# Routed experts: the steps between two arms move into the arms, and the arms are entered without hints

## The chip, the cores and the metric

The program runs on one core of one Trainium2 chip. The metric is the device time of one execution in microseconds (us), the median of several. The core has five engines, each with its own instruction stream: TensorE (PE in the rows; PEld is its loading of weights), VectorE (DVE), ScalarE (ACT), GpSimd (POOL) and SyncE (SP, here the engine that issues most DMAs). An engine takes its instructions in order and waits on semaphores for the others.

## What is computed

A trunk of two layers over 256 latent and 256 context tokens of width 1024: a recurrent mixer and a dense feed-forward network in the first layer, a pooling mixer and routed experts in the second. The change touches only the routed experts (latent tokens alone, each token goes to 2 of 8):

```python
def moe_swiglu(h, router_w, router_b, w1, w3, w2):
    logits = (h @ router_w) + router_b
    top_logit, top_idx = lax.top_k(logits, TOP_K)
    top_p = jax.nn.softmax(top_logit, axis=-1)
    gates = jnp.einsum('btk,btke->bte', top_p, jax.nn.one_hot(top_idx, N_EXPERTS))
    y = jnp.zeros_like(h)
    for e in range(N_EXPERTS):
        y = y + gates[..., e:e + 1] * swiglu(h, w1[e], w3[e], w2[e])
    return y
...
x = layer_norm(DN_ALPHA * x + gt2 * moe_swiglu(x * (1.0 + sc2) + sh2), ln_g, ln_b)
```

All data is float32. Each expert has 17.3 MB of weights (w1, w3: 1024 x 1408, w2: 1408 x 1024).

## The kernel before

The experts are worked one after the other. How many tokens an expert got is known only on the chip, so each expert is a switch with five arms: two blocks of up to 128 tokens, both full; a full and a small block (up to 64); one full block (`Full`); one small one (`Small`); one of up to 32 tokens (`Tiny`). The count, compared with 32, 64, 128 and 192, picks the arm. TensorE, VectorE, ScalarE and SyncE each load the number of the arm into a register and branch by themselves; each arm is its own stretch of code on each engine, and all arms of an expert are followed by one common block. With this input the experts 0, 4, 5 and 7 take the `Tiny` arm, 1, 2 and 6 the `Full` one, 3 the arm with a full and a small block.

Ahead of an arm stand three steps, which this text calls so:

- *gather*: 16 products of the normalised rows `z` with a one-hot matrix `oh` pick the expert's tokens, turned, into PSUM; eight affine steps (`affine3`, four on VectorE, four on ScalarE) bring them to `xg`.
- *turn*: two transposes and a copy make `ohT`, which the adding back needs.
- *adding back* (`scatter`): four products of `ohT` with the arm's result `yf`, and four additions with the gate on VectorE into `acc`.

The one-hot matrix of the next expert is made on GpSimd. In the kernel before these steps lie in the common block between two arms, in the order gather for e, turn for e, adding back of e - 1, then the branch into e's arm. `fetch` puts a hint behind the first instruction of the gather on each of three engines: it loads the register there and names the switch that will be taken (`tc.switch_hint`). SyncE has none. Every arm begins, in both kernels, with a hint for its own end.

An arm multiplies in 13 stages in the order `u0 u1 u2 d0 u3 d1 u4 d2 u5 d3 t5 d4 d5` (u: up, d: down, t: turning the last hidden piece). A full block multiplies in split form: data and weights are cut into a high and a low part of type fp32r, and three products (`mm3`, L237) take the place of one in float32. The weights are split while they are used: for each piece of 512 columns ScalarE makes the high part (L1284, `wh`) and VectorE the low one (L1285, `wl`), with four buffers each. The data are split in `begin` (`high`, `low`, into `xs3`). In the arm with one full block the first half of `u0` isn't split but multiplied in float32 (L1835), which the None in `split` does; `Tiny` (L1756, L1774) and `Small` (L1791, L1805) multiply in float32 throughout.

Weights come in pieces of 1 MB through 19 slots in a ring; SyncE issues the load of piece g + 19 when piece g has been used (`pload`). The scheduler of the language orders the instructions of one block of code on each engine, and doesn't move any across a branch.

Of the kernel before, what the change touches and what calls it, by code (L numbers as in the profile page):

```python
# [12 lines left out]
ALU = mybir.AluOpType  # L13
# [187 lines left out]
def kernel(ctx: ExitStack, tc: tile.TileContext, I: dict, out: bass.AP, dbg=None):  # L201
# [1076 lines left out]
    def split_weight(raw):  # L1278
# [9 lines left out]
        def at(a, o, n):  # L1288

            i = a * raw.shape[2] + o  # L1290
            return [v[:, i % PART:i % PART + n] for v in parts[i // PART]]
# [366 lines left out]
    def gather(oh, xg, n=P):  # L1658

        work = {}  # L1660
        for d4 in range(2):
            pt = gen()
            for j in range(4):
                dt = 4 * d4 + j
                for t in range(2):
                    i = nc.tensor.matmul(pt[:, P * j:P * j + n], lhsT=z[:, t, P * dt:P * dt + P], rhs=oh[:, t, 0:n], start=(t == 0), stop=(t == 1))  # L1666
                    work.setdefault(i.ins.engine, []).append(i.ins)
            for j in range(4):
                i = affine3(4 * d4 + j, xg[:, 4 * d4 + j], pt[:, P * j:P * j + n])
                work.setdefault(i.ins.engine, []).append(i.ins)  # L1670
        return work
# [22 lines left out]
    def fetch(e, work):  # L1694

        for g, w in work.items():
            n = len(nc.cur_bb.bb.instructions)
            tc.switch_hint({g: vals[e]}, len(BOUNDS) + 1, f"arm{e}")
            for i in list(nc.cur_bb.bb.instructions)[n:]:
                tc.add_manual_dep(i, w[0].name, S.same, reason="order")  # L1700
            for j in w[1:]:
                tc.add_manual_dep(j, i.name, S.same, reason="order")

    onehot(0, 0, nc.vector, oh)
    fetch(0, gather(oh, xgs[0]))
    turn_oh(oh, ohT[0])
    ex, p1_, sm = rt("ex", [P, 2, 1]), rt("p1_", [P, 2, 1]), rt("sm", [P, 2, 1])
# [105 lines left out]
    class Full(Block):  # L1813


        def high(self, sl):
            nc.scalar.activation(xs3[0][:, sl], self.xg[:, sl], AF.Copy)

        def low(self, sl):
            nc.vector.tensor_tensor(xs3[1][:, sl], self.xg[:, sl], xs3[0][:, sl], op=ALU.subtract)  # L1820

        def begin(self, two):
            for h in range(2):
                sl = slice(4 * h, 4 * h + 4)
                self.high(sl)
                if two or h:
                    self.low(sl)

        def up(self, c, sp):
            self.ps = gen()  # L1830
            ps = self.ps[:, 0:512 if c < 5 else 256]
            for k in range(DT):
                v = None if self.b else sp[c](k)
                if v is None:
                    nc.tensor.matmul(ps, lhsT=self.xg[:, k], rhs=self.w["u", c](k), start=(k == 0), stop=(k == DT - 1))  # L1835
                    if k == 3 and not self.b:
                        self.low(slice(0, 4))
# [255 lines left out]
```

## Time and profile before

| | us |
|---|---|
| median of 3 runs | 1413.09 |
| lowest, highest | 1411.98, 1415.58 |
| profiled execution | 1417.35 |
| its span, first to last instruction | 1415.5 |
| PE busy in the span | 1150.7 (81%) |
| DVE busy | 915.2 (65%) |
| ACT busy | 622.5 (44%) |
| POOL busy | 343.0 (24%) |

The profiled execution is a single one; its time stands 4.26 us above the median. A row of the trace gives the start in us from the beginning of the span, the duration, the engine, the line, what is written and read, and in brackets how long the engine had been idle before and what ended that. "issue" there means that the engine waited for nothing that the profile shows. Durations of single instructions overlap a little, so that x4 with 2.49 means one about every 0.62 us. The routed experts fill the span from about 944 to 1404 us.

### The profile page before, as it was taken

Reading aid. Unit: us, or ns where it says so; the run is one execution under the profiler, and the core shown is the slowest. Engines: PE = TensorE matmul, PEld = TensorE weight load, DVE = VectorE, ACT = ScalarE, POOL = GpSimd, SP = SyncE. Lnnn points to the kernel's source line nnn. Section 1 sums busy time; section 2 is a strip of 40 time slices with the busy share of each in tenths; the row PEclk is TensorE's granted clock in tenths of the full one; section 3 lists DMA queues with packets and bytes.
Section 4 is the critical chain, followed back from the end, with each engine's and each line's share of the span. In section 5 each row is a group of like instructions: output and inputs, shape, how many; then the busy total and the mean of one; then the engine's idle time right before and its main releaser. Section 6 shows DMA issues by size and latency. Waiting matters only on the chain.

```text
span 1415.5 us, 26008 instructions
## 1 busy us (share of the span) xinstructions
PE 1150.7 (81%) x9885; PEld 879.2 (62%) x9885; DVE 915.2 (65%) x1821; ACT 622.5 (44%) x1330; POOL 343.0 (24%) x467
## 2 busy tenths in 40 slices
PE   1589659977888788689689998957989899968886
PEld 0267448955566566554489898855768655646663
DVE  7897417857867776654977777662869545622764
ACT  3443218466655675221244444321758345311750
POOL 6341130037705667011622222050000000000000
PEclk8699879988967799589889999979999799998998
DMA  8225645566657446362935455739959354499950
GB/s 355 92 88 193 200 139 175 160 172 188 182 105 200 102 132 176 68 208 76 391 120 180 173 183 194 291 142 389 383 217 361 132 179 151 170 415 416 398 219 32
DMA packets 131594, 288.37 MB, mean 204 GB/s; under 512 B 63536, under 2 KB 90288, under 8 KB 108208
## 3 DMA queue, kind: packets, MB, share of 16 engines
q1 hardware_dynamic: 128064, 278.50, 56.4%
q10 hardware_dynamic: 3312, 7.31, 1.4%
q8 instruction: 95, 1.56, 0.5%
q14 instruction: 123, 1.01, 0.2%
HBM read 273.17 MB, written 12.60 MB: 202 GB/s over the span
## 4 chain that ended last, share of the span: by engine, by line
PE 38%; DVE 4%; DMA 4%; issue 3%; ACT 1%; POOL 0%; DVEq 0%; ACTq 0%; SPq 0%; POOLq 0%
PE pb L237 24%; PE pb L1756 3%; DMA arena<-in_moe_w13b_dram 3%; PE pb L1666 2%; PE pb L1791 2%; PE pb L1729 2%; PE pb L1835 1%; PE pb L1774 1%; DMA slot<-in_moe_w_dram 1%; PE pb L1805 1%; DVE wl L1285 1%; DVE usl L1433 1%; ACT wh L1284 0%; DVE x L1731 0%; DVE lnst L1360 0%
## 5 line engine op out<-in xcount | busy, mean ns | idle before, releaser
L1285 DVE TENSOR_TENSOR wl<-arena,wh 128x512 fp32r<-128x512 f32 x262 | 211.2, 832 | 77.7 <-ACT wh L1284 76.5
L1284 ACT ACTIVATE wh<-arena 128x512 fp32r<-128x512 f32 x262 | 160.3, 628 | 120.8 <-PE pb L237 106.7
L237 PE MATMUL pb<-usl,wh 128*128 128x256 f32 x352 | 101.0, 288 | 12.6 <-DVE usl L1433 12.6
L237 PE MATMUL pb<-ush,wh 128*128 128x256 f32 x352 | 100.0, 286 | 1.7 <-DVE fsg L1451 1.7
L237 PE MATMUL pb<-ush,wl 128*128 128x256 f32 x352 | 100.0, 285 | 0.0
L1656 POOL TENSOR_SCALAR oh<-consts,consts 128x128 f32<-128x128 f32 x14 | 8.3, 605 | 355.2 <-PE pb L1666 345.3
L1285 DVE TENSOR_TENSOR wl<-slot,wh 128x512 fp32r<-128x512 f32 x122 | 79.7, 687 | 22.3 <-ACT wh L1284 21.9
L1284 ACT ACTIVATE wh<-slot 128x512 fp32r<-128x512 f32 x122 | 75.0, 629 | 29.8 <-PE pb L237 26.6
L1097 DVE SCALAR_TENSOR_TENSOR sv<-sv,wc,pb 64x64 f32<-64x64 f32 x192 | 45.8, 278 | 57.9 <-issue 23.7
L1072 ACT ACTIVATE sv<-pb 64x128 f32<-64x128 f32 x128 | 34.6, 271 | 101.7 <-PE pb L1066 96.5
L237 PEld LDWEIGHTS pb<-usl,wh 128*128 128x128 f32 x352 | 68.2, 194 | 16.2 <-DVE usl L1433 14.0
L1315 POOL TENSOR_TENSOR arena<-arena,rows 128x2048 f32<-128x2048 f32 x11 | 52.0, 4729 | 103.8 <-DMA arena<-in_ffn_w_dram 103.8
L944 POOL TENSOR_TENSOR arena<-arena 128x56 f32<-128x56 f32 (+22 forms) x155 | 70.7, 456 | 12.2
L237 PEld LDWEIGHTS pb<-ush,wh 128*128 128x128 f32 x352 | 67.7, 193 | 4.0 <-DVE fsg L1451 1.9
L237 PE MATMUL pb<-wl,xsh 128*128 128x512 f32 (+1 forms) x180 | 69.7, 387 | 0.0
L237 PE MATMUL pb<-wh,xsh 128*128 128x512 f32 (+1 forms) x180 | 69.2, 387 | 0.0
L237 PEld LDWEIGHTS pb<-ush,wl 128*128 128x128 f32 x352 | 68.2, 194 | 1.2
L237 PE MATMUL pb<-wh,xsl 128*128 128x512 f32 (+1 forms) x180 | 67.0, 372 | 0.0
L1764 DVE TENSOR_TENSOR mh<-mh,pb 64x128 f32<-64x128 f32 (+1 forms) x24 | 7.0, 291 | 81.3 <-PE pb L1774 38.1
L853 PE MATMUL pb<-arena 128*128 128x192 f32 x256 | 52.3, 356 | 6.3 <-DVE arena L788 3.1
L853 PEld LDWEIGHTS pb<-arena 128*128 128x128 f32 x256 | 44.8, 204 | 11.3 <-DVE arena L788 3.8
L942 POOL TENSOR_TENSOR arena<-arena 128x126 f32<-128x126 f32 (+22 forms) x93 | 43.2, 464 | 27.8 <-DMA arena<-s 21.2
(446 smaller groups left out, 3089.0 us busy)
## 6 DMA issues: line engine op xcount, KB each, us to landing
slot<-in_moe_w_dram SPq DMA_DIRECT2D x62, 1024.0 KB, 11.2
arena<-in_moe_w_dram SPq DMA_DIRECT2D x58, 1024.0 KB, 6.7
arena<-in_ffn_w_dram SPq DMA_DIRECT2D x33, 1024.0 KB, 4.8
arena<-in_ada_w_dram SPq DMA_DIRECT2D x28, 512.0 KB, 4.3
ada<-in_ada_w_dram SPq DMA_DIRECT2D x28, 512.0 KB, 4.8
hvr<-in_w_rkv_dram SPq DMA_DIRECT2D x12, 1024.0 KB, 10.6
wr<-in_ada_w_dram SPq DMA_DIRECT2D x10, 1024.0 KB, 8.7
sv<-v_d SPq DMA_DIRECT2D x128, 64.0 KB, 2.8
```

Of the source, the lines that this page charges most:

```text
L237: i = nc.tensor.matmul(ps, lhsT=a[x], rhs=b[y], start=start and n == 0, stop=stop and n == 2)
L853: nc.tensor.matmul(pb(g)[:, 192 * j:192 * j + 192], lhsT=kap_b[kap.i][:, c + j].rearrange("p h t -> p (h t)"), rhs=kbi_b[kbi.i][:, c + j])
L942: eng.tensor_tensor(mv, T[:, cs, j:j + 1].to_broadcast([P, nci, nii]), X[:, ii, j].unsqueeze(1).to_broadcast([P, nci, nii]), op=ALU.mult)
L944: eng.tensor_tensor(T[:, cs, ii], T[:, cs, ii], mv, op=ALU.subtract)
L1072: nc.scalar.activation(sv_(si, d, 1)[zd(d)], bank[zd(d), 0:128], AF.Copy, scale=-1.0)
L1097: nc.vector.scalar_tensor_tensor(t[:, x], sv_(si, d, 0)[zd(d), x], wc_b[wc.i][zd(d), h, si:si + 1], bank[zd(d), 128 + 64 * h:192 + 64 * h] ...
L1284: nc.scalar.activation(hi, r[:, o:o + PART], AF.Copy)
L1285: nc.vector.tensor_tensor(lo, r[:, o:o + PART], hi, op=ALU.subtract)
L1315: S.behind(nc.gpsimd.tensor_tensor(w, w, gt.unsqueeze(1).to_broadcast(w.shape), op=ALU.mult))
L1666: i = nc.tensor.matmul(pt[:, P * j:P * j + n], lhsT=z[:, t, P * dt:P * dt + P], rhs=oh[:, t, 0:n], start=(t == 0), stop=(t == 1))
L1729: nc.tensor.matmul(ps, lhsT=ohT[:, t], rhs=yf[:, 512 * j:512 * j + 512], start=True, stop=True)
L1756: nc.tensor.matmul(ps[32 * g:32 * g + 32, 0:P], lhsT=xg[:, k, 0:32], rhs=m[g], start=(k == 0), stop=(k == DT - 1))
```

## The change

The common block between arms keeps only the register load and the branch, and the one-hot on GpSimd. Gather and turn for expert e + 1, and the splitting of its data (`halves`, now in every arm), stand in expert e's arm behind stage t5; adding back of e - 1 stands at the start of e's arm if that begins with a full block, else behind u1. All of `u0` is split, so the float32 product in single full arms goes. The three hints go.

```diff
     def gather(oh, xg, n=P):
 
-        work = {}
         for d4 in range(2):
...
             for j in range(4):
-                i = affine3(4 * d4 + j, xg[:, 4 * d4 + j], pt[:, P * j:P * j + n])
-                work.setdefault(i.ins.engine, []).append(i.ins)
-        return work
+                affine3(4 * d4 + j, xg[:, 4 * d4 + j], pt[:, P * j:P * j + n])
+
+    def halves():
+
+        for h in range(2):
+            sl = slice(4 * h, 4 * h + 4)
+            nc.scalar.activation(xs3[0][:, sl], xgs[0][:, sl], AF.Copy)
+            nc.vector.tensor_tensor(xs3[1][:, sl], xgs[0][:, sl], xs3[0][:, sl], op=ALU.subtract)
...
     onehot(0, 0, nc.vector, oh)
-    fetch(0, gather(oh, xgs[0]))
+    gather(oh, xgs[0])
     turn_oh(oh, ohT[0])
+    halves()
...
     def arm(e, kinds):
-        full, two = kinds[0] is Full, len(kinds) > 1
+        full, two, end = kinds[0] is Full, len(kinds) > 1, e == NE - 1
+        if full and e > 0:
+            scatter(e - 1, ohT[(e - 1) % 2])
...
-                ups[c] = parts_of([None if i == 0 and n == 0 and not two else split_weight(t) for n, t in enumerate(v)],
-                                  v[0].shape[1], v[0].shape[2])
+                ups[c] = parts_of([split_weight(t) for t in v], v[0].shape[1])
...
-        if full:
-            bl[0].begin(two)
...
+            if (a, c) == ("u", 1) and e > 0 and not full:
+                scatter(e - 1, ohT[(e - 1) % 2])
+            if a == "t" and not end:
+                gather(oh, xgs[0])
+                halves()
+                if not two:
+                    turn_oh(oh, ohT[(e + 1) % 2])
...
     for e in range(NE):
-
-        if e > 0:
-            fetch(e, gather(oh, xgs[0]))
-            turn_oh(oh, ohT[e % 2])
-            scatter(e - 1, ohT[(e - 1) % 2])
         if e + 1 < NE:
             onehot(e + 1, 0, nc.gpsimd, oh)
-        for k in tc.Switch({g: vals[e] for g in ARM_ENGINES}, len(ARMS), hint=f"arm{e}"):
+        for k in tc.Switch({g: vals[e] for g in ARM_ENGINES}, len(ARMS)):
             arm(e, ARMS[k])
```

What the scheduler made of it, first on TensorE between the arms of experts 1 and 2. The rows are the program's own order, with PSUM banks as `pb`; SWITCH_STRIDE and ISA work out the target. Before:

```order
L1677 MATMUL pb_64<-consts,oh 128x128 x2
L1666 MATMUL pb_70<-oh,z_8187 128x128
L1698 SWITCH_STRIDE
L1693 TENSOR_LOAD cnt
L1698 ISA
L1698 BRANCH_PREFETCH_HINT
L1666 MATMUL pb_70<-oh,z_8187 128x128 x7
L1666 MATMUL pb_63<-oh,z_8187 128x128 x8
L1729 MATMUL pb_69<-yf,consts_5875 128x512
L1729 MATMUL pb_64<-yf,consts_5875 128x512
L2089 SWITCH_STRIDE
L2089 ISA x2
```

The same place of the changed kernel, from the end of expert 1's last arm to the head of expert 2's first:

```order
L1769 MATMUL pb_67<-slot_8099,consts 32x256 x4
L2071 UNCONDITIONAL_BRANCH
L1697 TENSOR_LOAD cnt
L2071 SWITCH_STRIDE
L2071 ISA x2
L1934 BRANCH_PREFETCH_HINT
```

Turn (L1677), gather (L1666), adding back (L1729) and the hint are gone from between the arms; the register load now stands directly ahead of the branch. The hint that is left is the arm's own, for its end.

VectorE at the head of expert 2's full arm, before (`xsl` is the low half of the data):

```order
L1952 BRANCH_PREFETCH_HINT
L1820 TENSOR_TENSOR xsl<-xg,xsh 128x512 x2
L1285 TENSOR_TENSOR wl<-slot_8505,wh 128x512 x4
L1285 TENSOR_TENSOR wl<-slot_8507,wh 128x512 x4
L1844 TENSOR_TENSOR mh<-mh,pb_63 128x256
```

And now:

```order
L1934 BRANCH_PREFETCH_HINT
L1285 TENSOR_TENSOR wl<-slot_8483,wh 128x512 x3
L1726 SCALAR_TENSOR_TENSOR x_8262<-pb_69,consts,x_8262 128x512
L1285 TENSOR_TENSOR wl<-slot_8483,wh 128x512
L1726 SCALAR_TENSOR_TENSOR x_8262<-pb_70,consts,x_8262 128x512
L1726 SCALAR_TENSOR_TENSOR x_8262<-pb_63,consts,x_8262 128x512
L1726 SCALAR_TENSOR_TENSOR x_8262<-pb_64,consts,x_8262 128x512
L1285 TENSOR_TENSOR wl<-slot_8485,wh 128x512 x4
```

Up to the end of the first up product there stood two low halves of the data and four low parts of weights; now there are eight low parts and the four additions of the adding back.

VectorE at the end of the same arm, before:

```order
L1285 TENSOR_TENSOR wl<-slot_8096,wh 128x512 x4
L1855 TENSOR_TENSOR hh1l<-pb_70,hh1h 128x128
L1285 TENSOR_TENSOR wl<-slot_8097,wh 128x512 x2
L1871 TENSOR_TENSOR yf<-pb_65,gt 128x512
L1871 TENSOR_TENSOR yf<-pb_66,gt 128x512
```

And now (`xg` and `xsl` belong to expert 3):

```order
L1285 TENSOR_TENSOR wl<-slot_8096,wh 128x512 x4
L1834 TENSOR_TENSOR hh1l<-pb_64,hh1h 128x128
L1653 TENSOR_SCALAR xg<-pb_70,raa,rab 128x128
L1285 TENSOR_TENSOR wl<-slot_8097,wh 128x512
L1653 TENSOR_SCALAR xg<-pb_70,raa,rab 128x128
L1285 TENSOR_TENSOR wl<-slot_8097,wh 128x512
L1850 TENSOR_TENSOR yf<-pb_65,gt 128x512
L1675 TENSOR_TENSOR xsl<-xg,xsh 128x512
L1850 TENSOR_TENSOR yf<-pb_66,gt 128x512
```

The affine steps and a low half stand between the last parts of the weights and between the two scalings of the arm's result.

## Rows read from the trace of the kernel before

**Rows 1.** Busy time by stretch: expert 1's full arm behind its first product.

```profile
core 0: us, PE busy (x) PEld busy (x) DVE busy (x) ACT busy (x) POOL busy (x), PEclk, DMA share, GB/s
1001.50:1043.21 41.71, 41.71 (x202) 34.64 (x201) 40.03 (x70) 36.85 (x68) 0.00 (x0) 1.00 0.96 360
```

**Rows 2.** The same view, from an arm's last product to the next's first, experts 1 to 7.

```profile
975.73:992.65 16.92, 9.45 (x42) 6.75 (x43) 6.12 (x12) 3.63 (x8) 1.19 (x2) 0.88 1.01 410
1043.21:1057.05 13.84, 7.85 (x42) 4.89 (x41) 5.04 (x10) 4.14 (x9) 1.18 (x2) 0.99 0.36 130
1106.14:1120.94 14.80, 8.97 (x43) 5.08 (x41) 5.48 (x12) 5.33 (x11) 1.18 (x2) 0.79 0.35 122
1224.62:1235.51 10.89, 7.69 (x42) 4.98 (x41) 5.30 (x10) 2.21 (x5) 1.18 (x2) 1.00 0.33 125
1256.99:1272.94 15.95, 8.17 (x42) 5.12 (x43) 5.85 (x12) 2.11 (x5) 1.19 (x2) 0.96 1.01 412
1296.90:1313.96 17.06, 9.34 (x42) 6.64 (x43) 6.11 (x12) 4.01 (x9) 1.19 (x2) 0.87 1.01 411
1364.28:1376.77 12.49, 7.91 (x43) 4.91 (x41) 5.04 (x10) 2.11 (x5) 0.00 (x0) 1.00 0.17 55
```

**Rows 3.** The chain that ended last, first products of full arms: start, us, what.

```profile
992.65 6.70 PE pb L1835 x8
...
1057.05 5.22 PE pb L1835 x8
...
1068.24 5.50 PE pb L237 x24
...
1313.96 6.47 PE pb L1835 x8
```

**Rows 4.** Timeline, TensorE's first product in an arm, experts 0, 1, 2, 4, 5, 6.

```profile
953.95 3.70 PE L1756 MATMUL pb<-arena,xg 128*32 128x128 f32 x128 [1.91 <-ACT xg L1651]
...
992.65 2.90 PE L1835 MATMUL pb<-slot,xg 128*128 128x512 f32 x3 [5.45 <-issue]
...
1057.05 5.22 PE L1835 MATMUL pb<-slot,xg 128*128 128x512 f32 x8 [3.28 <-issue]
...
1235.51 3.70 PE L1756 MATMUL pb<-slot,xg 128*32 128x128 f32 x128 [3.02 <-issue]
...
1272.94 6.45 PE L1756 MATMUL pb<-slot,xg 128*32 128x128 f32 x128 [5.54 <-issue]
...
1313.96 2.90 PE L1835 MATMUL pb<-arena,xg 128*128 128x512 f32 x3 [5.78 <-issue]
```

**Rows 5.** Timeline, ScalarE's first instruction in the arms of experts 1 and 2.

```profile
991.24 1.15 ACT L1817 ACTIVATE xsh<-xg 128x512 fp32r<-128x512 f32 x2 [5.21 <-issue]
...
1055.02 1.15 ACT L1817 ACTIVATE xsh<-xg 128x512 fp32r<-128x512 f32 x2 [2.42 <-issue]
```

**Rows 6.** Timeline, first instruction behind an arm: after experts 0, 1, 4, 6.

```profile
977.43 0.44 PE L1677 MATMUL pb<-consts,oh 128*128 128x128 f32 x2 [1.71 <-issue]
...
1049.46 0.41 DVE L1652 TENSOR_SCALAR xg<-pb,raa,rab 128x128 f32<-128x128 f32 x1 [5.39 <-PE pb L1729]
...
1263.09 0.41 DVE L1652 TENSOR_SCALAR xg<-pb,raa,rab 128x128 f32<-128x128 f32 x1 [4.22 <-issue]
...
1369.42 0.41 DVE L1652 TENSOR_SCALAR xg<-pb,raa,rab 128x128 f32<-128x128 f32 x1 [4.27 <-PE pb L1729]
```

**Rows 7.** Timeline, durations of the moved steps around experts 1 and 5.

```profile
975.90 1.77 DVE L1780 TENSOR_TENSOR yf<-pb,gt 32x256 f32<-32x256 f32 x4 [2.27 <-DMA arena<-in_moe_w_dram]
...
983.40 3.80 PE L1729 MATMUL pb<-yf,consts 128*128 128x512 f32 x8
...
985.45 1.48 DVE L1731 SCALAR_TENSOR_TENSOR x<-pb,consts,x 128x512 f32<-128x512 f32 x2
...
994.58 2.49 DVE L1285 TENSOR_TENSOR wl<-slot,wh 128x512 fp32r<-128x512 f32 x4
...
1259.72 3.60 PE L1666 MATMUL pb<-oh,z 128*128 128x128 f32 x30 [0.32 <-issue]
```

More of the change, by code (lines that the diff above doesn't have):

```diff
@@ L1288, in at @@
         def at(a, o, n):
+            n = n or raw.shape[2]
             i = a * raw.shape[2] + o
@@ L1665, in gather @@
                 for t in range(2):
-                    i = nc.tensor.matmul(pt[:, P * j:P * j + n], lhsT=z[:, t, P * dt:P * dt + P], rhs=oh[:, t, 0:n], start=(t == 0), stop=(t == 1))
-                    work.setdefault(i.ins.engine, []).append(i.ins)
+                    nc.tensor.matmul(pt[:, P * j:P * j + n], lhsT=z[:, t, P * dt:P * dt + P], rhs=oh[:, t, 0:n], start=(t == 0), stop=(t == 1))
             for j in range(4):
-                i = affine3(4 * d4 + j, xg[:, 4 * d4 + j], pt[:, P * j:P * j + n])
-                work.setdefault(i.ins.engine, []).append(i.ins)
-        return work
+                affine3(4 * d4 + j, xg[:, 4 * d4 + j], pt[:, P * j:P * j + n])
[4 more added lines that the diff above has]
+            nc.vector.tensor_tensor(xs3[1][:, sl], xgs[0][:, sl], xs3[0][:, sl], op=ALU.subtract)
     def turn_oh(oh, ohT):
@@ L1693 @@
     vals = [nc.values_load(cnt[0:1, e:e + 1], engines=ARM_ENGINES, min_val=0, max_val=len(BOUNDS)) for e in range(NE)]
[L1694 to L1702, printed above, removed]
     onehot(0, 0, nc.vector, oh)
-    fetch(0, gather(oh, xgs[0]))
+    gather(oh, xgs[0])
     turn_oh(oh, ohT[0])
+    halves()
     ex, p1_, sm = rt("ex", [P, 2, 1]), rt("p1_", [P, 2, 1]), rt("sm", [P, 2, 1])
@@ L1813 @@
     class Full(Block):
[L1816 to L1827, printed above, removed]
         def up(self, c, sp):
@@ L1832, in up @@
             for k in range(DT):
-                v = None if self.b else sp[c](k)
-                if v is None:
+                if self.b:
                     nc.tensor.matmul(ps, lhsT=self.xg[:, k], rhs=self.w["u", c](k), start=(k == 0), stop=(k == DT - 1))
-                    if k == 3 and not self.b:
-                        self.low(slice(0, 4))
                 else:
-                    mm3(ps, [x[:, k] for x in xs3], v, k == 0, k == DT - 1)
+                    mm3(ps, [x[:, k] for x in xs3], sp[c](k), k == 0, k == DT - 1)
         def act(self, c):
@@ L1874, in rows_of, with parts_of @@
         return lambda k: v[k // v[0].shape[1]][:, k % v[0].shape[1]]
-    def parts_of(v, m, n):
-        return lambda k: v[k // m] and v[k // m](k % m, 0, n)
+    def parts_of(v, m):
+        return lambda k: v[k // m](k % m, 0, None)
     def arm(e, kinds):
-        full, two = kinds[0] is Full, len(kinds) > 1
+        full, two, end = kinds[0] is Full, len(kinds) > 1, e == NE - 1
+        if full and e > 0:
+            scatter(e - 1, ohT[(e - 1) % 2])
         if two:
@@ L1935, in arm @@
             scatter(e, ohT[(e + 1) % 2])
+            if not end:
+                turn_oh(oh, ohT[(e + 1) % 2])
         bl[0].end()
```

## The prediction

> **What bounds the kernel now.** I read the page first, then cut the routed stage into stretches, then followed each engine across the stretches between two arms. The page's shares of busy time are means over the whole span and say nothing about this change, which touches only the last third.
>
> The cut shows two regimes. Inside a full arm, from the end of its first up product to the end of its last down product, TensorE is busy 41.71 of 41.71 us, and VectorE is close behind with 40.03 [rows 1]. Whatever TensorE is given there is added to the time, and VectorE has under 2 us to spare. Between the last product of one arm and the first product of the next lie 11 to 17 us, in which TensorE works about 8 us (gathering, turning, adding back) and waits for the rest [rows 2]. In the first such stretch after a full arm it waits 13.84 - 7.85 = 6.0 us. The eighth stretch, ahead of the first arm, is only the 1.9 us of the entry itself [rows 4].
>
> What the waits are made of: an engine that enters an arm waits for nothing the profile names. TensorE does so for 3.0 to 3.3 us in the four entries after arms with a full block (two are shown), but for 5.5 to 5.8 us in the three after small-count (Tiny) arms [rows 4]; ScalarE for 2.42 and 5.21 us in the same two cases [rows 5]. Both kinds were hinted. Leaving an arm costs too: VectorE's first work after a full arm comes 5.39 us after its last, at another place 4.27, after a Tiny arm 4.22 with "issue" as the reason [rows 6]. TensorE leaves a Tiny arm in 1.7 us [rows 6], a full one without a gap. In the kernel before, VectorE's exit runs beside TensorE's gather; that is its cover.
>
> The first product of a full arm takes 5.2 to 6.7 us for its unsplit half, where 24 split products (a whole up product) take 5.50 [rows 3], so half would take 2.75.
>
> **The change part by part.** TensorE's work is only moved: gather and turn are 7.85 - 3.80 = 4.05 us, adding back is 3.80 [rows 2, 7]. It leaves stretches in which TensorE waits anyhow, and goes into arms in which it doesn't.
>
> *Entry without a hint.* No row shows one. From below it is what the cheap entries cost, 3.1 us on TensorE and 2.4 on ScalarE; from above, what the dear ones cost, 5.6 and 5.2 [rows 4, 5]. I take the dear level: VectorE's exits, branches whose target evidently wasn't there, cost 4.2 to 5.4 even where the DMA queues were nearly idle (share 0.17 at the 4.27) [rows 2, 6]. The register load that used to stand at the hint now stands at the entry; TensorE paused 0.32 us for it and the hint together [rows 7], so 0.3 more: 5.9 on TensorE, 5.5 on the other two.
>
> [...]
>
> *Exit and entry in a row.* Between arms there is now nothing but the load and the branch, so on VectorE the exit (4.9 after full, 4.2 after Tiny) and the entry (5.5) add up, with nothing running beside them: about 10 us. Who waits for VectorE: the split of the next full arm's first weights, and through it TensorE.
>
> *Entering a full arm (experts 1, 2, 6).* VectorE now makes eight low parts at 0.62 us and four additions at 0.74 before the first product can end [rows 7], 8.0 us, and the last three products take 0.7. After a full arm: 0.9 (the scalings behind the last product end 5.39 us ahead of 1049.46, 0.86 after 1043.21 [rows 2, 6]) + 4.9 + 5.5 + 8.0 + 0.7 = 20.0 us from last product to end of first product; before it was 13.84 + 5.2 + 2.75 = 21.8 [rows 2, 3]. Gain 1.8. After a Tiny arm: 2.5 (four scalings, 1.77 [rows 7], and a low half, 0.7) + 4.2 + 5.5 + 8.0 + 0.7 = 20.9, against 26.4 and 26.3. Gain 5.5 and 5.4. Adding back on TensorE (3.80) lies inside VectorE's wait and costs nothing; if VectorE came 5 us sooner, TensorE would be next, at 5.9 + 3.8 + 5.5 = 15.2 after a full arm.
>
> *Inside the full arms.* 4.05 us more on TensorE each. Besides, VectorE starts the second product without the lead of four parts that the slow first half gave it, and its 40.0 us grow by four affine halves and two low halves, about 3, to 43 of 46. I add 1.0 for waits. So +5.0 for each of three arms. The arm with two blocks (expert 3) already split everything and is TensorE's throughout: +4.05.
>
> *Entering the others.* Expert 3: VectorE must come first (its one-hot): 0.9 + 4.9 + 5.5 + 0.5, and its four additions now stand ahead of the block's affine steps, 1.3: 13.1 against 14.80, gain 1.7. Expert 4: TensorE alone, 5.9 against 10.89, gain 5.0. Expert 5: 1.7 + 5.9 against 15.95, gain 8.3. Expert 7: 5.9 against 12.49, gain 6.6. In these VectorE's late arrival (11 to 12 us after the last product) is covered by the next arm's first products and the adding back, which now follow the entry. Expert 0: 5.9 against 1.92, loss 4.0: there the hinted entry was wholly hidden behind ScalarE.
>
> *Inside the Tiny arms.* Gather and turn 4.05 and adding back 3.80, less some 0.6 that fills small waits: expert 0 +3.4, 4 and 5 +7.3 each, 7 (no gather) +3.8.
>
> *Clock.* After 5.5 us of waiting the first 128 matmul records of a Tiny arm took 6.45 us, after 3.0 us only 3.70 [rows 4]. Expert 4 changes from the second case to the first; I take half of the 2.75, 1.4.
>
> *At nothing.* Weight loads: TensorE waits for none of them in these arms, they keep their order, and arms get longer, which gives them more time. The two splitting steps in Tiny arms that need none: both engines are mostly idle there; without that cover 2.5 us each.
>
> **Sum.** Entries: +4.0 - 5.5 - 1.8 - 1.7 - 5.0 - 8.3 - 5.4 - 6.6 = -30.3. Arms: 3.4 + 3 x 5.0 + 4.05 + 2 x 7.3 + 3.8 = +40.9. With the clock +12.0 us. The profiled execution took 1417.35 us (span 1415.5), so 1429 by its own measure; it lies 4.3 above the median of 1413.09, for which I predict **1425**. 0.3%, or 4.2 us, is what a measurement can tell from no change.
>
> **The rivals.**
> 1. *The hints bought nothing*, and an entry keeps the price of its place: what divides the levels is that the weight queues are full (share 1.01) at the dear ones and a third full or less at the cheap ones [rows 2]. Then expert 0 loses 3.7 less, the two entries bound by VectorE 2.8 less each, experts 4 and 7 2.5 less each, and the clock term goes: 12.0 - 15.7 = -3.7, 1409. Against it: expert 0's cheap entry came with full queues. [...] 0.2.
> 2. *Faster:* the dear entries are the hint's own doing, since only entries after short arms are dear, where the hint comes close behind another one; without hints all cost the cheap level. Then the entries of experts 1, 5 and 6 give 8 more: -12, 1401. It decides as soon as an entry costs TensorE under about 3.6 us on the mean over eight. Against it: the exits show branches at 4.2 to 5.4. 0.08.
> 3. *Slower still:* a fetch behind full queues costs another step of 2.8 (the gap between the levels) in experts 0, 1, 5 and 6: +11, 1436; or VectorE becomes the bound of the full arms, +2 each. 0.12.
>
> **How the numbers follow.** My forecast 0.55 (1418 to 1435), the rivals 0.2, 0.08 and 0.12, and 0.05 for a mixture that ends within the bound. Rival 1 lies on the border; I give 0.08 of it to faster and 0.12 to no change. Faster 0.16, the same 0.17, slower 0.67. The range for 8 in 10 goes from 1408 to 1437.
>
> **What would show it.** Right: TensorE's entries of experts 2, 4 and 7 at 5 us or more; VectorE's gap between the last scaling of a full arm and the next arm's first low part about 10 us; full arms of 46 us from first product's end to last product; no product of L1835's kind in single full arms. Wrong: entries near 3 us (rival 1 or 2), or VectorE's exit shrinking to under 2 us because the block behind the arms is now so short, which alone would give some 10 us back until TensorE bounds the entry.

## The result and the profile after

The changed kernel took 1422.0 us (median of 20 runs, 1414.76 to 1427.54), the kernel before 1413.95 us on the same chips (20 runs): the ratio is 1.0055, with a 95% interval from 1.0039 to 1.0072. So it is slower, by some 8 us. The profiled execution took 1420.72 us, its span is 1418.9 us. Its page, busy time by engine and one of the two queues of kind instruction (packets, MB, share), q8, which the run with longer code below ties to TensorE's code (98 packets with three more products in each single full arm, 95 without them):

```profile
PE 1147.9 (81%) x9897; PEld 880.9 (62%) x9897; DVE 925.3 (65%) x1841; ACT 630.1 (44%) x1350; POOL 344.6 (24%) x467
...
q8 instruction: 98, 1.61, 0.5%
```

TensorE has as much to do as before (1147.9 us against 1150.7), VectorE 10 us more, ScalarE 8. Busy time by stretch, in the order of [rows 1, 2]: two full arms from the last product of `u0` on, then from an arm's last product to TensorE's first product of the next.

```profile
core 0: us, PE busy (x) PEld busy (x) DVE busy (x) ACT busy (x) POOL busy (x), PEclk, DMA share, GB/s
1004.56:1049.78 45.22, 45.22 (x232) 37.86 (x230) 41.35 (x76) 38.58 (x75) 1.45 (x2) 1.00 0.90 336
1068.15:1113.31 45.16, 45.16 (x232) 37.84 (x230) 41.45 (x76) 38.60 (x75) 1.45 (x2) 1.00 0.89 338
979.51:996.59 17.08, 5.91 (x9) 2.32 (x9) 5.15 (x10) 3.11 (x6) 0.90 (x2) 0.75 1.02 401
1049.78:1062.44 12.66, 5.46 (x8) 2.15 (x9) 3.93 (x8) 2.19 (x4) 0.14 (x1) 0.73 0.28 95
1113.31:1126.28 12.97, 6.00 (x9) 2.37 (x8) 4.23 (x10) 2.19 (x4) 0.14 (x1) 0.74 0.28 92
1228.57:1234.11 5.54, 0.01 (x1) 0.04 (x2) 0.86 (x2) 0.00 (x0) 0.00 (x0) 0.97 0.51 180
1262.64:1269.56 6.92, 0.01 (x2) 0.03 (x1) 2.37 (x5) 0.93 (x2) 0.90 (x2) 0.88 1.01 397
1301.26:1319.04 17.78, 5.81 (x10) 2.24 (x9) 5.16 (x10) 3.12 (x6) 0.90 (x2) 0.81 1.01 402
1371.37:1377.57 6.20, 0.00 (x0) 0.03 (x1) 1.23 (x3) 0.00 (x0) 0.00 (x0) 0.69 0.33 100
```

The full arms are 45.2 us long, with TensorE busy throughout. Into experts 4, 5 and 7 the way has become short, as the moved steps are gone from it. Into the full arms (experts 1, 2, 6) it is as long as before, 17.1 against 16.9 us, 12.7 against 13.8, 17.8 against 17.1 [rows 2], though the gather and the turning have left it. The last stretch is the way into expert 7; the one ending at 1126.28 leads into expert 3, whose first product is the gather of its second block. The waits there, TensorE's timeline:

```profile
986.88 5.91 PE L1724 MATMUL pb<-yf,consts 128*128 128x512 f32 x8 [7.37 <-issue]
996.59 0.77 PE L237 MATMUL pb<-wh,xsh 128*128 128x512 f32 x1 [3.80 <-DVE x L1726]
...
1056.06 5.46 PE L1724 MATMUL pb<-yf,consts 128*128 128x512 f32 x8 [6.28 <-issue]
1062.44 0.47 PE L237 MATMUL pb<-wh,xsh 128*128 128x512 f32 x1 [0.92 <-DVE x L1726]
1119.84 5.99 PE L1724 MATMUL pb<-yf,consts 128*128 128x512 f32 x8 [6.53 <-issue]
1126.28 3.79 PE L1666 MATMUL pb<-sct,z 128*128 128x64 f32 x32 [0.45 <-DVE x L1726]
1234.11 5.17 PE L1751 MATMUL pb<-slot,xg 128*32 128x128 f32 x128 [5.54 <-DMA slot<-in_moe_w_dram]
...
1307.96 5.80 PE L1724 MATMUL pb<-yf,consts 128*128 128x512 f32 x8 [6.70 <-issue]
1319.04 0.73 PE L237 MATMUL pb<-wh,xsh 128*128 128x512 f32 x1 [5.27 <-DVE x L1726]
```

TensorE waits 5.5 to 7.4 us between any two arms; into experts 4 and 5 the profile names a weight transfer as what ended the wait (5.54 and 6.92 us), elsewhere nothing. Where a full arm follows it then adds back, in 5.5 to 6.0 us where this took 3.80 before [rows 7] (the granted clock of these stretches is 0.73 to 0.81, over the adding back alone 0.61 to 0.67; over the 3.80 us it was 1.00), and waits again, until VectorE has made the first addition, whose bank the first product takes. VectorE, its first work in the arms of experts 1 and 2, and ScalarE, in those of experts 1, 2 and 6:

```profile
993.77 1.89 DVE L1285 TENSOR_TENSOR wl<-slot,wh 128x512 fp32r<-128x512 f32 x3 [11.59 <-ACT wh L1284]
...
1059.74 1.89 DVE L1285 TENSOR_TENSOR wl<-slot,wh 128x512 fp32r<-128x512 f32 x3 [8.73 <-issue]
...
993.05 2.19 ACT L1284 ACTIVATE wh<-slot 128x512 fp32r<-128x512 f32 x4 [12.59 <-PE pb L1724]
...
1056.26 2.19 ACT L1284 ACTIVATE wh<-slot 128x512 fp32r<-128x512 f32 x4 [6.83 <-issue]
...
1315.49 2.19 ACT L1284 ACTIVATE wh<-arena 128x512 fp32r<-128x512 f32 x4 [13.28 <-issue]
```

ScalarE, which has nothing to do between the arms, needs 6.8 us for exit and entry behind a full arm, and 12.6 and 13.3 behind Tiny ones, where the weight queues are full (share 0.28, and 1.02 and 1.01, in the stretches above). For the 12.6 a product of TensorE is named, for the 13.3 nothing, and in the run that moves the adding back behind `u1` the same two waits are 12.8 and 13.2 us. Full queues and a Tiny arm ahead always come together here, so that no run tells which of them makes the difference.

From one arm's last product to the next one's, by expert (differences of the stretches' edges here and in [rows 2]; for expert 0 from the router's first product, which starts at 941.63 before and 940.64 after; the last arm ends at 1396.30 and 1400.81):

| expert | 0 | 1 | 2 | 3 | 4 | 5 | 6 | 7 | sum |
|---|---|---|---|---|---|---|---|---|---|
| before | 34.1 | 67.5 | 62.9 | 118.5 | 32.4 | 39.9 | 67.4 | 32.0 | 454.7 |
| after | 38.9 | 70.3 | 63.5 | 115.3 | 34.1 | 38.6 | 70.1 | 29.4 | 460.2 |
| change | +4.8 | +2.8 | +0.6 | -3.2 | +1.7 | -1.3 | +2.7 | -2.6 | +5.5 |
| predicted | +7.4 | -0.5 | +3.2 | +2.4 | +3.7 | -1.0 | -0.4 | -2.8 | +12.0 |

The sums belong to one execution each. In the profiled executions below the router's first product starts anywhere from 935 to 945 us, though nothing ahead of it was changed; so the table is the finer view of the routed stage, and the medians are the verdict. A single column isn't finer than some 2 us: expert 0's, whose code is the same in the changed kernel and in those with the adding back between the arms, is 38.9 us here and 36.9 and 38.9 us there.

### The profile page after: what moved, and what is told of

Its sections match the earlier page's. It is cut to its first block, busy times and chain, and to the rows that moved or that the text cites. A ratio compares the mean times of both kernels' runs of the same rounds, so it can differ in the third digit from the quotient of the medians.

```text
span 1418.9 us, 25963 instructions
## 1 busy us (share of the span) xinstructions
PE 1147.9 (81%) x9897; PEld 880.9 (62%) x9897; DVE 925.3 (65%) x1841; ACT 630.1 (44%) x1350; POOL 344.6 (24%) x467
## 3 DMA queue, kind: packets, MB, share of 16 engines
q10 hardware_dynamic: 3312, 7.31, 1.4%
q8 instruction: 98, 1.61, 0.5%
q14 instruction: 124, 1.02, 0.3%
## 4 chain that ended last, share of the span: by engine, by line
PE 37%; DVE 6%; issue 5%; DMA 4%; ACT 2%; SPq 0%; DVEq 0%; POOL 0%; ACTq 0%; POOLq 0%
PE pb L237 24%; PE pb L1751 3%; PE pb L1666 2%; PE pb L1786 2%; PE pb L1769 1%; DVE wl L1285 1%; DMA bpool<-in_consts_dram 1%; PE pb L1724 1%; DMA arena<-in_ffn_w_dram 1%; ACT wh L1284 1%; PE pb L1800 1%; DMA slot<-in_moe_w_dram 1%; DMA rows<-in_lnrows_dram 1%; DVE usl L1434 1%; DMA arena<-in_lnrows_dram 0%
## 5 line engine op out<-in xcount | busy, mean ns | idle before, releaser
L1284 ACT ACTIVATE wh<-arena 128x512 fp32r<-128x512 f32 x266 | 162.0, 628 | 135.9 <-PE pb L237 100.1
L237 PE MATMUL pb<-usl,wh 128*128 128x256 f32 x352 | 101.7, 289 | 12.6 <-DVE usl L1434 12.6
L1285 DVE TENSOR_TENSOR wl<-slot,wh 128x512 fp32r<-128x512 f32 x130 | 84.5, 686 | 38.8 <-ACT wh L1284 29.8
L1284 ACT ACTIVATE wh<-slot 128x512 fp32r<-128x512 f32 x130 | 79.3, 628 | 59.0 <-PE pb L237 28.9
L237 PE MATMUL pb<-ush,wl 128*128 128x256 f32 x352 | 100.8, 287 | 1.8 <-DVE wl L1285 1.8
L237 PE MATMUL pb<-ush,wh 128*128 128x256 f32 x352 | 100.7, 288 | 1.8 <-DVE fsg L1452 1.8
L237 PE MATMUL pb<-wh,xsh 128*128 128x512 f32 (+1 forms) x192 | 74.6, 394 | 10.0 <-DVE x L1726 10.0
L237 PEld LDWEIGHTS pb<-usl,wh 128*128 128x128 f32 x352 | 68.9, 196 | 16.2 <-DVE usl L1434 14.0
L237 PE MATMUL pb<-wl,xsh 128*128 128x512 f32 (+1 forms) x192 | 76.2, 397 | 0.0
L237 PE MATMUL pb<-wh,xsl 128*128 128x512 f32 (+1 forms) x192 | 73.1, 381 | 0.0
L237 PEld LDWEIGHTS pb<-ush,wh 128*128 128x128 f32 x352 | 68.5, 196 | 4.1 <-DVE fsg L1452 2.0
L237 PEld LDWEIGHTS pb<-ush,wl 128*128 128x128 f32 x352 | 69.0, 196 | 3.2 <-DVE wl L1285 2.0
L1724 PE MATMUL pb<-yf,consts 128*128 128x512 f32 x72 | 42.7, 735 | 28.3 <-issue 26.9
L853 PEld LDWEIGHTS pb<-arena 128*128 128x128 f32 x256 | 46.2, 209 | 10.4 <-DVE slotsw L869 2.7
```

The source lines that it names most:

```text
L237: i = nc.tensor.matmul(ps, lhsT=a[x], rhs=b[y], start=start and n == 0, stop=stop and n == 2)
L853: nc.tensor.matmul(pb(g)[:, 192 * j:192 * j + 192], lhsT=kap_b[kap.i][:, c + j].rearrange("p h t -> p (h t)"), rhs=kbi_b[kbi.i][:, c + j])
L1284: nc.scalar.activation(hi, r[:, o:o + PART], AF.Copy)
L1285: nc.vector.tensor_tensor(lo, r[:, o:o + PART], hi, op=ALU.subtract)
L1724: nc.tensor.matmul(ps, lhsT=ohT[:, t], rhs=yf[:, 512 * j:512 * j + 512], start=True, stop=True)
```

## The experiments

All ratios are to the kernel before, measured on the same chip, with 95% intervals in brackets; the changed kernel stands at 1.0055.

**The hints.** The kernel before without them:

```diff
...
-            fetch(e, gather(oh, xgs[0]))
+            gather(oh, xgs[0])
...
-        for k in tc.Switch({g: vals[e] for g in ARM_ENGINES}, len(ARMS), hint=f"arm{e}"):
+        for k in tc.Switch({g: vals[e] for g in ARM_ENGINES}, len(ARMS)):
```

> The kernel before, with the three hints per expert taken out and nothing else moved; the register load then stands at the branch. Theory (a hint is worth the step between the cheap and the dear entries): TensorE's entries behind full arms, in experts 2, 3, 4 and 7, go from 3.0 to 3.3 us to about 6, those behind Tiny arms stay at 5.5 to 5.8; the hint's own 0.3 us go: four times 2.8 less eight times 0.3, +9 us, or +12 if expert 0's entry shows too. Rival 1 of the prediction (the hints bought nothing, the place sets the price): no entry grows, -2 to 0 us. The opposite rival (a hint close behind another one makes the entry dear): the entries of experts 1, 5 and 6 fall to about 3 us, -8 us or more.

1416.06 us, ratio 0.9995 (0.9973 to 1.0017). TensorE's first products in the arms of experts 1, 2, 4 and 7:

```profile
989.80 6.24 PE L1825 MATMUL pb<-slot,xg 128*128 128x512 f32 x8 [6.04 <-issue]
...
1054.22 6.46 PE L1825 MATMUL pb<-slot,xg 128*128 128x512 f32 x8 [3.31 <-issue]
...
1234.40 5.10 PE L1746 MATMUL pb<-slot,xg 128*32 128x128 f32 x128 [3.38 <-issue]
...
1377.69 2.58 PE L1746 MATMUL pb<-arena,xg 128*32 128x128 f32 x44 [3.32 <-issue]
```

The entries are what they were with hints [rows 4], within 0.6 us, except expert 0's, which went from 1.91 to 3.03 us. (The routed stage of this one execution is 4.2 us longer than in the profile before, which the medians of 12 and 35 runs don't bear out.) So the hints bought nothing that shows, and losing them is not what the change lost by.

**The split half alone.** The kernel before with all of `u0` split:

```diff
...
-                ups[c] = parts_of([None if i == 0 and n == 0 and not two else split_weight(t) for n, t in enumerate(v)],
-                                  v[0].shape[1], v[0].shape[2])
+                ups[c] = parts_of([split_weight(t) for t in v], v[0].shape[1], None)
```

> The kernel before, with the first half of u0 of single full arms in split form; hints, gather, turning and adding back stay where they were. Theory: the slow half product goes (2.5 to 3.9 us of TensorE in each of three arms) but VectorE's eight low parts take its place as what ends last, and the second product loses its lead: -1 us an arm, -3 us in all (-6 to 0). If TensorE alone counted: -9 us. If VectorE, 40 of 41.7 us busy, bounds the arm: 0 to +3 us.

1414.21 us, ratio 0.9984 (0.996 to 1.0008): no change that can be told. The -2.3 us of the ratio lie within the theory's range, and far from the -9 of TensorE alone; the interval, -5.7 to +1.1 us, doesn't exclude the 0 of the third reading.

**The adding back, later in the arm.** The changed kernel, with single full arms adding back behind `u1`:

```diff
-        if full and e > 0:
+        if two and e > 0:
             scatter(e - 1, ohT[(e - 1) % 2])
...
-            if (a, c) == ("u", 1) and e > 0 and not full:
+            if (a, c) == ("u", 1) and e > 0 and not two:
                 scatter(e - 1, ohT[(e - 1) % 2])
```

> The changed kernel, with the adding back of single full arms behind u1 (as in the other arms) and no longer at the arm's start. In the changed kernel's trace the first split product of these arms waits 0.9, 3.8 and 5.3 us, and ends on an addition. Theory: without the additions there the first product starts some 2 us sooner in the arms of experts 1 and 6 and 1 us sooner in expert 2's: -4 to -6 us against the changed kernel. Rival: the waits are for the low parts, which come as late, or the additions cost as much of VectorE later in the arm: 0 us against the changed kernel.

1422.15 us, ratio 1.0052 (1.0032 to 1.0072), the same as the changed kernel. The rival holds: the first split product then waits for ScalarE's part instead: the page puts 10.9 us of waiting of these products (L237, `wh,xsh`) down to `ACT wh L1284`, where the changed kernel's puts 10.0 down to `DVE x L1726`.

**The adding back between the arms again,** with hints and without:

```diff
-        if full and e > 0:
-            scatter(e - 1, ohT[(e - 1) % 2])
...
-            if (a, c) == ("u", 1) and e > 0 and not full:
-                scatter(e - 1, ohT[(e - 1) % 2])
...
     for e in range(NE):
+        if e > 0:
+            scatter(e - 1, ohT[(e - 1) % 2])
```

> The changed kernel, with the adding back between the arms again and a hint behind its first product and first addition (on ScalarE ahead of the branch); gather, turning and splitting of the data stay in the arms. Theory: the adding back covers a part of VectorE's exit and gives the hint 3 to 5 us of lead, so TensorE's entries behind full arms are back at about 3 us; entries and adding back together take 7.7 us in experts 4 and 7, 12 in expert 5: about 8 to 10 us faster than the changed kernel, 0 to -2 against the kernel before. Rival: the lead is too short or the hint bought nothing, and entries stay at 6 to 7 us: as slow as the changed kernel, or slower by the adding back, which no longer lies beside VectorE's entry (+0 to +4).

> The changed kernel with the adding back between the arms again, and this time without hints. Theory (what an entry costs is set by how much queued work lies over it, and hints play no part): as fast as with hints, 1414 us, or 1 to 2 us faster by the hints' own time; TensorE's exit behind full arms again 2.9 us, and its entries under 2 us where it alone counts. If the hints did the work there: entries back at 6 us, 1420 or more.

With hints 1414.46 us, 1.0005 (0.998 to 1.0031); without 1413.47, 1.0003 (0.998 to 1.0026). The loss is gone, and the hints make no difference again: the first run came out as its theory said, but not by the lead that this gave the hints. Without hints, the way into experts 2 and 5, and expert 4's first product:

```profile
1049.03 5.26 PE L1724 MATMUL pb<-yf,consts 128*128 128x512 f32 x8 [3.26 <-issue]
...
1058.84 0.62 PE L237 MATMUL pb<-wl,xsh 128*128 128x512 f32 x1 [4.10 <-DVE wl L1285]
...
1235.38 3.70 PE L1751 MATMUL pb<-slot,xg 128*32 128x128 f32 x128 [1.40 <-DMA slot<-in_moe_w_dram]
...
1270.45 5.36 PE L1751 MATMUL pb<-slot,xg 128*32 128x128 f32 x125 [2.33 <-DMA arena<-in_moe_w13b_dram]
```

TensorE's exit from a full arm is now seen by itself (3.26 us), then comes the adding back. Into experts 4 and 5 the wait behind it is 1.4 and 2.3 us, with a weight transfer named. Full arms still start late: the first part on VectorE is what the second of the three split products waits for (4.10 us).

By expert, measured as in the table above, the routed stage is 8.2 us shorter than in the changed kernel, 7.2 of them in the Tiny arms of experts 4, 5 and 7 (3.2, 1.1 and 2.9). Expert 3 is 3.7 longer, and the full arms change by -2.3, +1.6 and -2.0 (expert 0, with the same code, by -2.0).

**The same with the first half in float32 again:**

```diff
...
-                ups[c] = parts_of([split_weight(t) for t in v], v[0].shape[1])
+                ups[c] = parts_of([None if i == 0 and n == 0 and not two else split_weight(t) for n, t in enumerate(v)], v[0].shape[1])
```

> As the run before it (adding back between, no hints), with the first half of u0 of single full arms in float32 again, so that TensorE's first product needs nothing that ScalarE and VectorE make in the new arm. Where that half was split TensorE waited 7.0 + 1.3 us in expert 1, 3.9 in expert 2 and 6.9 + 1.3 in expert 6 for the first parts. Theory: with an entry of 3 to 4 us behind the adding back the float32 half starts some 3 us earlier and lasts 5 to 6.5 us instead of 2.75, while the parts of the second half are made beside it: -3 us in experts 1 and 6, -1 in expert 2, 1407 to 1409 us in all, the best so far. Rival: TensorE's own entry is as late as ScalarE's, and the slow half is added in full: +3 an arm, 1423.

1394.35 us, ratio 0.9865 (0.983 to 0.9899): the fastest kernel of this study, and better than was expected. TensorE into expert 2, and that way as a stretch:

```profile
1043.64 3.67 PE L1724 MATMUL pb<-yf,consts 128*128 128x512 f32 x8 [0.78 <-DVE xsl L1675]
1049.20 3.67 PE L1817 MATMUL pb<-slot,xg 128*128 128x512 f32 x8 [1.89 <-DVE x L1726]
```

```profile
core 0: us, PE busy (x) PEld busy (x) DVE busy (x) ACT busy (x) POOL busy (x), PEclk, DMA share, GB/s
1042.86:1049.20 6.34, 3.67 (x9) 1.47 (x9) 2.41 (x5) 0.00 (x0) 0.14 (x1) 1.00 0.54 180
```

From the last product of one arm to the first of the next lie 6.34 us *with* the adding back in them. In the changed kernel 6.28 us passed without it, and the adding back came on top. So it is behind arms with a full block: into experts 4 and 7 the way with the adding back is 6.4 and 7.1 us, without it 5.5 and 6.2. Behind Tiny arms it is hardly covered: into experts 1, 5 and 6 the way is 10.6, 10.6 and 9.7 us with it and 7.4, 6.9 and 6.7 without. The granted clock is 1.00 on the way into expert 2; the adding back takes 3.67 us there and the float32 half 3.67 instead of 5.22 [rows 3], over which it was 0.70. By expert, the run is 15.6 us shorter than the one before it in experts 1, 2 and 6 together and 1.1 in expert 3; the others lie within some 2 us.

**The adding back alone into the arms,** of the kernel before:

```diff
-            scatter(e - 1, ohT[(e - 1) % 2])
         if e + 1 < NE:
...
+        if full and e > 0:
+            scatter(e - 1, ohT[(e - 1) % 2])
...
+            if (a, c) == ("u", 1) and e > 0 and not full:
+                scatter(e - 1, ohT[(e - 1) % 2])
```

> The kernel before with the adding back alone moved into the arms, as in the change; gather, turning and hints stay between the arms. Theory (either step is cover enough for an exit; only with nothing at all between the arms do exit and entry add up): the adding back costs its 3.8 us in the arm and gives them between the arms, -2 to +3 us against before, with TensorE's exits and entries as before. Rival (the move of the adding back is itself what costs: in the arm it stands in VectorE's way and in the cold stretch of TensorE): +6 to +8 us, as much as the change did.

1405.71 us, ratio 0.9939 (0.9917 to 0.9961): faster, which neither had expected. Into expert 2:

```profile
1045.81 5.19 PE L1729 MATMUL pb<-yf,consts 128*128 128x512 f32 x8 [4.79 <-ACT xg L1651]
1051.72 3.70 PE L1835 MATMUL pb<-slot,xg 128*128 128x512 f32 x8 [0.72 <-DVE x L1731]
```

The gather begins without a gap behind the arm, as before, so that no exit shows. The slow stretch behind the wait falls on the adding back (5.19 us), and the float32 half runs in 3.70 where it took 5.22 [rows 3].

**Work for nothing between the arms.** The changed kernel with products of the identity, whose result nobody reads:

```diff
     for e in range(NE):
+        if e > 0:
+            keep_warm(32)
```

> The changed kernel with 32 products of the identity with itself (128x128, into a free bank, result unused) on TensorE between every two arms, as much work as a gather. Theory (exit and entry of an engine are each hidden by the work queued over them, and TensorE's two stand bare in a row): the 3.6 us of added work cost nothing in experts 2, 3, 4, 5 and 7, since TensorE's idle time before the arm falls by as much, and the adding back and the first products behind it run at the full clock: 0 to -8 us against the changed kernel. Rival (an exit and an entry in a row cost what they cost, whatever else is queued): 7 times 3.6, +20 to +25 us.

1431.37 us, ratio 1.0129 (1.0093 to 1.0165). The products took 7.31 us, not 3.6: a gather has 16 products and not 32. Into expert 2:

```profile
1046.82 7.31 PE L1312 MATMUL pb<-consts 128*128 128x128 f32 x64
1056.25 3.67 PE L1724 MATMUL pb<-yf,consts 128*128 128x512 f32 x8 [2.13 <-issue]
```

Seven times 7.31 are 51 us of added work; the time grew by about 9 (1431.37 against 1422.0; by the ratios, 0.74%, 10). They begin without a gap, so that no exit shows, and 7.31 + 2.13 = 9.4 us take the place of 6.28; the adding back is 1.8 us faster behind them. By expert, the full arms take -1.3, +0.4 and -0.8 us against the changed kernel, expert 3 1.9 more, and the Tiny arms of experts 4, 5 and 7 4.8, 2.7 and 3.6 more. The forecast of no cost was wrong in size; that most of the added work is covered, all of it ahead of full arms, holds.

**The first half in float32, and nothing else undone:** the edit of the 1394 us kernel, in the changed one, with the adding back at the head of the arm, and then behind `u1`. Besides the line with `split_weight` (and `parts_of`, which passes the None on) it takes these in `Full.up`:

```diff
-                if self.b:
+                v = None if self.b else sp[c](k)
+                if v is None:
                     nc.tensor.matmul(ps, lhsT=self.xg[:, k], rhs=self.w["u", c](k), start=(k == 0), stop=(k == DT - 1))
                 else:
-                    mm3(ps, [x[:, k] for x in xs3], sp[c](k), k == 0, k == DT - 1)
+                    mm3(ps, [x[:, k] for x in xs3], v, k == 0, k == DT - 1)
```

> The changed kernel with nothing undone but the splitting of u0's first half in single full arms, which is one float32 product of eight steps again; gather, turning, splitting of the data and adding back stay in the arms, no hints. Theory A (the split half is what the change lost by: its first product waits for parts that ScalarE and VectorE can only make after their own exit and entry): a gain of 5 to 6 us an arm as between the runs with the adding back outside, 1403 to 1406 us. Theory B (with the adding back at the arm's head the first product waits for an addition in any case, since it takes the bank that this one reads, so the half starts as late and is slower by 2.5 us, with some of the parts made beside it): -1 to +2 an arm, 1419 to 1428.

> As the run before it, with the adding back of single full arms behind u1, so that the first product of these arms meets neither a part nor an addition. If theory B holds there, this run gives what that one could not: some 6 us an arm against the changed kernel, 1402 to 1406. If theory A holds there, this run is the same as that one within 2 us.

At the head 1422.74 us, 1.0061 (1.0036 to 1.0085); behind `u1` 1414.4 us, 0.9989 (0.9966 to 1.0012). Theory B holds at the head: in expert 6 the half waits 4.51 us for an addition (1313.58). Behind `u1`, expert 2's first product:

```profile
1050.93 6.04 PE L1817 MATMUL pb<-slot,xg 128*128 128x512 f32 x8 [6.50 <-issue]
```

The wait for an addition is gone, and 8 us come back, half of what was expected, so that neither forecast for this run holds. What stays lost against the 1394 us kernel lies in part in the adding back, which the arm pays for, and in the slow start: 6.04 us for the half (granted clock 0.60) instead of 3.67.

**Other banks for the first two products of the adding back,** in the 1394 us kernel:

```diff
-    def scatter(e, ohT):
+    def scatter(e, ohT, free=()):
...
-                ps = gen()
+                ps = free[j] if free and t == 0 else gen()
...
-            scatter(e - 1, ohT[(e - 1) % 2])
+            scatter(e - 1, ohT[(e - 1) % 2], accb[2 * (e % 2):2 * (e % 2) + 2])
```

> The fastest kernel so far (adding back between the arms, no hints, first half unsplit, 1394 us), with the first two products of the adding back going to the two accumulator banks that the next arm doesn't use before d0, so that the next arm's first product finds a bank that no addition has to release. In that kernel TensorE's first products waited 4.9, 1.9, 2.4 and 2.7 us (experts 1, 2, 6, 7) with an addition named as what ended it. Theory (VectorE's exit makes the additions late, and the bank hands it on to TensorE): 1 to 2 us less at each of these entries, -4 to -8 us, 1386 to 1390. Rival (TensorE's own entry ends no earlier): 0 us.

1398.46 us, 0.9874 (0.9846 to 0.9902): no different. Expert 2's first product waits 1.82 us for nothing named, where it waited 1.89 for an addition, and expert 6's 2.37 where it waited 2.36. There the name had been that of the event that came last; the entry itself ended no earlier. Of the four waits only expert 1's fell, from 4.88 to 3.24 us.

**Longer code.** The 1394 us kernel with three identity products more in each single full arm:

```diff
             if a == "t" and not end:
+                if full and not two:
+                    keep_warm(3)
                 gather(oh, xgs[0])
```

> The kernel of 1394 us (adding back between, first half unsplit) with three identity products more in each arm of one full block, behind t5, their result unused: 0.7 us of TensorE an arm, 2 us in all. What it is for: the page's queue q8, of kind instruction, moved 95 packets in the kernel before and in the 1394 us kernel, but 98 in the changed kernel and in both runs with the adding back between and the half split, three more, as many as there are arms with one full block; and TensorE's exit from these arms cost 0.8 us in the 1394 us kernel and 3.3 where the half was split. Theory (the length of TensorE's code in a full arm, which the split half adds to, makes its exit dear): 98 packets again, exits behind experts 1, 2 and 6 near 3 us, the adding back behind them at 5.3 us, so 4 us an arm and the products: +10 to +16 us, 1404 to 1410. Rival (the split half itself is what costs, through the parts that come late): 95 or 98 packets, exits at 0.8 us, +2 us, 1396.

1401.93 us, 0.9925 (0.9898 to 0.9953). The page, and the adding back behind experts 1 and 2:

```profile
q8 instruction: 98, 1.61, 0.5%
```

```profile
1041.49 3.67 PE L1724 MATMUL pb<-yf,consts 128*128 128x512 f32 x8 [2.94 <-issue]
...
1100.01 3.67 PE L1724 MATMUL pb<-yf,consts 128*128 128x512 f32 x8 [0.77 <-DVE xsl L1675]
```

The packets rose from 95 to 98 as the theory said, but only one exit of three became dear. So three more packets are not three dear exits. The ratio rose by 0.6%, some 8 us, for 2 us of added work, the routed stage of the profile by 3.5 us; what makes the exit 0.8 us in one place and 3 in another stays open. It is a warning too: a few unread products move the time by as much as some of the differences below.

The runs side by side, as ratios to the kernel before, by where the steps stand (hints, which make no difference, left aside):

| gather and turning | adding back | first half float32 | first half split |
|---|---|---|---|
| between | between | 1 (before) | 0.9984 |
| between | in the arm | 0.9939 | not run |
| in the arm | between | **0.9865** | 1.0003 |
| in the arm | in the arm, at its head | 1.0061 | **1.0055** (the change) |
| in the arm | in the arm, behind `u1` | 0.9989 | 1.0052 |

## Why the prediction was right, and where it was wrong

The sign was right, the size near (+12.0 forecast against +8 in the medians and +5.5 in the routed stage of the two profiles), and all four signs it named showed: entries of 5.5 us or more in experts 2, 4 and 7, VectorE's gap of 8.7 us, full arms of 45 us, no float32 half. But the cause it gave for the dear entries was wrong, and sizes that were wrong in both directions cancelled: the forecast was 9 us too low at the entries of experts 1 and 6, and some 15 too high in experts 0, 3 and 4, at expert 2's entry and inside the full arms. That the total came out near is in part luck.

- **"Entry without a hint. ... I take the dear level."** This step failed. Hints show no worth here (0.9995, 0.9973 to 1.0017), so the first rival's premise was right. But its conclusion, entries at their old price, was wrong too: TensorE waited 6.28, 6.53 and 6.21 us into experts 2, 3 and 7, near the 5.9 forecast, where before it waited 3.0 to 3.5. What is new there is that exit and entry stand in a row with no queued work over them, and with 3.67 us of adding back between them the way into expert 2 still took 6.34 us. What an engine waits for where the profile names nothing, whether a branch's target "wasn't there" as the prediction has it, and why a hinted entry costs as much as an unhinted one, no run here shows.
- **"Exit and entry in a row"** was worked out for VectorE alone and was right in kind: 8.73 us measured behind full arms for 10.4. That it holds for TensorE too was not seen, as the rows of before show no gap at TensorE's exit from a full arm, where the gather follows. (The prediction read its entries behind arms with a full block as four of 3.0 to 3.3 us with nothing named; expert 3's was 3.50 us and ended on VectorE's one-hot.)
- **"Adding back on TensorE (3.80) lies inside VectorE's wait and costs nothing"** holds nearly, for the kernel as it was predicted. TensorE came at 6.3 to 7.4 us and added back in 5.5 to 6.0 in the slow stretch (granted clock 0.61 to 0.67), and yet putting it back between the arms gave the three full arms only 2.7 us in all while the half was split; most of the 0.5% came from the Tiny arms. With the half unsplit the same move gave 2%, and 5.6, 5.6 and 9.1 us in the full arms.
- **Entering full arms after Tiny ones:** 5.5 and 5.4 us of gain were forecast for experts 1 and 6, and 0.9 and 1.0 came (last product to the start of `u0`'s last): behind Tiny arms, with full weight queues (share 1.02 and 1.01), ScalarE's two branches took 12.6 and 13.3 us instead of 6.8. This is the place and the sign of the third rival's price step, at twice its 2.8 us, but on ScalarE; TensorE's waits there grew by 1.1 us at most. Into expert 2 the gain was 3.1 us, for 1.8.
- **Full arms, +5.0 each:** 3.7 (45.2 us against 41.5 from the last product of `u0` in the trace of before); TensorE stayed busy throughout, so VectorE did not become the bound.
- **Expert 3, +4.05 in the arm:** the way into it gained 1.8 as forecast (1.7), but the arm itself got 1.4 us shorter (118.48 to 115.26 us in all). The slow stretch behind the wait now lies on the adding back (5.99 us at a granted clock of 0.61), and the second block's gather and turning take 4.0 us at 1.00, where they took 7.3 at 0.50. That is 3.3 of the 5.4 us missed; the rest stays open.
- **Expert 0, -4.0 for the entry:** the entry cost 0.4 us (12.7 us from the router's first product to the arm's, 12.3 before), the wait before it grew from 1.91 to 4.08 us, but gather and turning ahead of it took 1.8 us less; why they did stays open. Its arm lost 4.4, of which 1.7 is the first 128 products in the slow stretch (5.37 us for 3.70, granted clock 0.68 for 1.00).
- **Tiny arms:** experts 4, 5 and 7 came within 2 us of their forecast. Weight loads, put at nothing, are named at the entries of experts 4 and 5; what they add there is not shown.

What made the change slow is thus shown by the runs as to its parts: moving the gather and the turning brings 1.35%, and either of the other two, the adding back in the arm (0.9989 or 1.0061) or the split first half (1.0003), takes this gain away. How they do so is read from the traces. With the adding back gone too, nothing is left between two arms, and exit and entry stand bare in a row (5.5 to 7.4 us of TensorE's waiting); the split first half hands TensorE's start to the two engines that come latest (4.10 us of waiting for VectorE's first part into expert 2, with the adding back between the arms). Differences of some 0.5%, as the change's own loss against the kernel before, are no larger than what a few unread products moved in the run with longer code, so that where the code lies may have a share in them; no run separates that.

## What to carry to other kernels

Leave work between two branches that the engines can queue: behind expert 1's full arm it took 6.3 us from the last product to the next arm's first, with and without 3.7 us of useful work in it; behind short arms this didn't hold (9.7 to 10.6 us with it, 6.7 to 7.4 without), so measure it in each place. Let the first product behind an entry need nothing that another engine must first make in the new arm (0.9865 so, and 1.0003 with the split half). When a change is made of several moves, run the table of their combinations: here two moves gained 1.35% and 0.6% singly and nothing together (0.9989 and 1.0061).

## What was not expected of the hardware

- Two branches in a row cost ScalarE 6.8 us with the DMA queues at a share of 0.28 and 12.6 to 13.3 at 1.01 to 1.02, with no instruction of its own between them. The second case is always that behind a Tiny arm, so that the queues as the cause are not shown.
- A stretch of waiting is paid twice: after 6.5 us of it eight float32 products took 6.04 us (granted clock 0.60), after 1.9 us 3.67. What stands first behind such a wait takes that loss (with the adding back first, 5.19 us for it and 3.70 for the half behind it, which took 5.22 where it stood first), so a step that is on nobody's path should stand there. The length of the wait alone doesn't decide: after 3.0 us the first 128 products of a Tiny arm of the kernel before took 3.70 us in expert 4 (granted clock 1.00) and 5.37 in expert 7 (0.68).
- Instruction packets of the queue q8 went from 95 to 98 with TensorE's code in a full arm longer by three products, three for three arms run; 1.61 MB in 98 packets are 16.4 KB each on the mean. The other instruction queue's 124 packets in the changed kernel, 1.02 MB, are 8.2 KB each.
